# Output projections: the residual by plain loads and VectorE adds, and the linear attention's second block in the order of its first

## The chip, the cores and the metric

One core of a Trainium2 chip. The time of a kernel is device microseconds (us) of one execution of the whole program. The kernel before was run three times; its median is the time before. One further execution was taken by the hardware profiler, and everything said of the inside of the kernel is from that one. The engines are named as in the profile: PE (TensorE, matrix products; PEld is its loading of the stationary operand), DVE (VectorE), ACT (ScalarE), POOL (GpSimd) and SP (SyncE, which here only issues transfers).

## The reference

A decoder trunk of two layers for one sequence of 256 tokens, width 2048, all in float32. The first layer is a gated linear attention, the second a block-sparse attention (MoBA) over a shared K and V; behind each stands a gated convolutional FFN of hidden width 5632. Cut to what matters:

```python
def reference(x, ...):
    h = x
    for layer in range(2):
        if layer < 1:
            h = h + gla_mixer(h, ...)      # ends with  o.reshape(B, S, 2048) @ w_out
        else:
            k_blk, v_blk, k_mean = shared_kv(h, ...)
            h = h + moba_mixer(h, ...)     # ends with  o @ w_out
        h = h + conv_ffn(h, ...)           # ends with  (silu(a) * u) @ w_down
    return h
```

The change concerns the two products `@ w_out`, each of 256 x 2048 by 2048 x 2048, and the addition of `h` (the residual) to their results.

## The kernel before, in words

**Products.** A weight matrix is streamed from HBM in chunks of 1 MB (128 partitions x 2048 floats). SP issues the loads; the chunks go into three buffers (`raw`, tile `wraw`). Each chunk is split, in pieces of 1024 columns, into a high part (`whi`, a cast by ScalarE, L140) and a low part (`wlo`, a subtraction by VectorE, L141), both in the type that TensorE multiplies at full pace. The activations have been split in the same way. A product of two split numbers takes three matmuls: high x high, low x high and high x low. A `wraw` buffer is free for the next load only when the last cast and the last subtraction that read it are done. `WeightStream.prefetch` makes splits and loads a few pieces ahead of their use.

**Output and down projections (`down`, L702).** There are four: "go" (linear attention), "dn0", "mo" (MoBA) and "dn1". Each goes over two column blocks `b` of 1024 outputs. In a block, the 2048 (or 5632) inputs come as pairs of 128-row tiles, one chunk of weights for each pair. A pair is done in one of two ways:

- *plain*: 24 matmuls of 128x512, straight from the chunk's two wide pieces;
- *seven-product* (a `+` in the order): a 2x2 block scheme with 7 instead of 8 products, so 21 matmuls. Its chunk has four pieces: `b11` (half width), `wide`, and two sums of blocks, `t13` and `t24`, which VectorE computes first in three operations (`_sums`, L106 to L108; 1024, 512 and 512 elements a row), and which are then split like the other pieces. It also needs combined activations (`comb`).

The order of the pairs in each block stands in a table, `ORDERS`; what comes behind the bar is the block's *tail* of three plain pairs (20 and 21 pairs have theirs likewise in "dn0" and "dn1"). The matrix in HBM is packed in the order of the table.

Eight accumulators hold the partial results. At the last seven-product pair, five of them are merged into four tiles `r[0]` to `r[3]` (`c0` to `c3`, L756 to L760). In "go" and "mo" two of the others (`p[2]` and `p[3]`) are the halves of one accumulator pair (`acc`), and two (`p[4]` and `p[8]`) have a bank each. The tail runs twice over its three pairs: first for the column half `f = 0` (`p[2]`, `p[4]`), then for `f = 1` (`p[3]`, `p[8]`). Behind each half two results are added to their `r` (L771), and `done` (L781) takes the finished tile: a store (L784, GpSimd's queue), its squares for the next norm (L317, ScalarE), and later its transposes by TensorE (L795).

**The residual.** Right after the merge, four loads on GpSimd's queue add the residual to `r[0]` to `r[3]` in memory (L762, `accum_op=OP.add`): in "go" from `x_tok`, in "mo" from `rows2`, in the down projections from `rows1` and `rows3`. Each is 128 x 512 floats, 256 KB.

**What sets the order.** The program is written as one sequence; the framework's scheduler (switched on by `schedule_with_timeline_sim=True`) puts each engine's instructions in a fixed order before the run, and on the chip every engine and every queue works strictly in that order. `ws.behind()` keeps an instruction behind the latest split pieces. A moved dependency can so change the order on several engines around it.

Of the kernel before, what the change touches and what calls it, by code (L numbers as in the profile page):

```python
# [8 lines left out]
F32 = mybir.dt.float32  # L9
# [3 lines left out]
OP = mybir.AluOpType  # L13
# [24 lines left out]
def _order(text):  # L38

    words = text.replace("|", " ").split()  # L40
    return [(int(k.rstrip("+")), k.endswith("+")) for k in words], len(text.split("|")[1].split())
# [1 line left out]

EARLY = (1, 3, 5, 7)
ORDERS = {
    "go": [_order("0 1+ 2 3+ 4 | 5 6 7"), _order("0 2 1+ 3+ 4 | 5 6 7")],
    "dn0": [_order("0 2 4 6 8 1+ 10 3+ 12 5+ 14 7+ 16 9+ 17 11+ 18 13+ 15 | 19 20 21"),
            _order("0 2 4 6 1+ 8 3+ 10 5+ 12 7+ 14 9+ 16 11+ 13+ 18 15+ 17+ 19 | 20 21")],
    "mo": [_order("0 2 1+ 3+ 4 | 5 6 7"), _order("0 2 1+ 3+ 4 | 5 6 7")],
# [108 lines left out]
def trunk(ctx: ExitStack, tc: tile.TileContext, xT, x_tok, cst, msk, w1p, w2a, w_k, w_qa, w_v2, w_v, w_g, w_go,  # L158
          w_up0, w_dn0, w_kk, w_kv, w_mq, w_mo, w_up1, w_dn1, rel, onehot, out):
    nc = tc.nc  # L160
    V, A, T = nc.vector, nc.scalar, nc.tensor
# [11 lines left out]
    def slot(shape, dt, name):  # L173
        return big.tile(shape, dt, name=name, tag="slot")

    def temp(name, shape=(128, 2, S), dt=F32):
        return tmp.tile(list(shape), dt, name=name, tag="temp")

    def bank(name, shape):
        return mis_ps.tile(list(shape), F32, name=name, tag="bank")  # L180
# [5 lines left out]
    ws = WeightStream(tc, raw, parts)  # L186
# [85 lines left out]
    def step():  # L272
        due = [job for at, job in later if at <= cur[0]]
        later[:] = [(at, job) for at, job in later if at > cur[0]]
        for job in due:
            job()
        halves_ = ws.get(cur[0])
        cur[0] += 1
        return halves_
# [331 lines left out]
    def combine_parts(k, xs, into):  # L611
        t = temp("whole")
        V.tensor_add(t, xs[k][:, :, :S], xs[k][:, :, S:])
        combine(k, [(t[:, i, :128], t[:, i, 128:]) for i in range(2)], into)
# [4 lines left out]
    go, go_sums = [], {}  # L619
# [81 lines left out]

    def down(name, xs, combos, res, done, jobs):  # L702

        for b, (order, n_tail) in enumerate(ORDERS[name]):
            new = [k for k, seven in order if seven and k not in combos]
            todo = {i: list(js) for i, js in jobs.get(b, {}).items()}
            for k in new:
                at = next(i for i, (k_, _) in enumerate(order) if k_ == k)
                todo.setdefault(max(at - 2, 0), []).append(lambda k=k: combine_parts(k, xs, combos))
            low = acc_ps.tile([128, 2, 512], F32, name="acc")  # L710
            pair, single = ((3, 8), (2, 4)) if name.startswith("dn") else ((2, 3), (4, 8))
            p = {n: low[:, i] for i, n in enumerate(pair)}
            p.update({n: bank(f"p{n}", (128, 512)) for n in single})
            left = dict.fromkeys(range(1, 9), 0)
            for k, seven in order:
                for n in ((1, 5, 7, 6, 4, 3, 2) if seven else (2, 3, 4, 8, 2, 3, 4, 8)):
                    left[n] += 3
            begun = set()

            def prods(*todo):  # L720

                w = step()
                for n, _, _ in todo:
                    if n not in p:
                        two = acc_ps.tile([128, 2, 512], F32, name="acc")
                        p.update({n: two[:, 0], {1: 6, 5: 7}[n]: two[:, 1]})
                for xi, wi in ((0, 0), (1, 0), (0, 1)):
                    for n, x, f in todo:
                        left[n] -= 1
                        T.matmul(p[n], x[xi], w[wi][:, 512 * f:512 * f + 512], start=n not in begun, stop=left[n] == 0)  # L730
                        begun.add(n)

            def part(k, i, t):
                x = xs[k][:, i, 128 * t:]
                return x[:, :128], x[:, S:S + 128]

            def comb(k, f):
                return combos[k][:, f, 0], combos[k][:, f, 1]

            last = max(i for i, (k, seven) in enumerate(order) if seven)  # L740
            for i, (k, seven) in enumerate(order[:-n_tail]):
                for job in todo.get(i, ()):
                    job()
                if seven:
                    prods((1, part(k, 0, 0), 0))
                    prods((3, comb(k, 3), 0), (2, part(k, 1, 0), 1))
                    prods((5, comb(k, 0), 0), (7, comb(k, 2), 1))
                    prods((6, comb(k, 1), 0), (4, part(k, 1, 1), 1))
                else:
                    for a in range(2):  # L750
                        prods(*((n, part(k, a, t), f)
                                for n, t, f in ((2, 0, a), (3, 0, 1 - a), (4, 1, a), (8, 1, 1 - a))))
                if i == last:

                    r = [temp(f"c{n}", (128, 512)) for n in range(4)]
                    A.copy(r[0], p[1])  # L756
                    V.tensor_add(r[1], r[0], p[6])  # L757
                    V.tensor_add(r[2], r[1], p[7])
                    V.tensor_add(r[1], r[1], p[5])
                    V.tensor_add(r[3], r[2], p[5])  # L760
                    for n in (0, 2, 1, 3):
                        nc.gpsimd.dma_start(r[n], res(n // 2, 2 * b + n % 2), accum_op=OP.add)  # L762
            for f, ns in enumerate(((2, 4), (3, 8))):
                for i, (k, _) in enumerate(order[-n_tail:]):
                    for job in todo.get((f, i), ()):
                        job()
                    prods(*((n, part(k, a, t), a) for a in range(2) for t, n in enumerate(ns)))
                if f:
                    ws.prefetch(cur[0])
                for t, n in enumerate(ns):  # L770
                    V.tensor_add(r[2 * t + f], r[2 * t + f], p[n])  # L771
                    done(t, 2 * b + f, r[2 * t + f])
# [41 lines left out]
    def middle(name, xs, combos, res, nrm, keep_row, at, feature_major, parked=None):  # L814
        done, back, in_acc, in_bank = onward(nrm, keep_row, parked)
        jobs = {}
        for q, (b, i) in enumerate(at):
            jobs.setdefault(b, {}).setdefault(i, []).append(lambda q=q: back(q, in_acc))
        down(name, xs, combos, res, done, jobs)
        for q in range(len(at), NP):  # L820
            after(1 if feature_major else q - 3, lambda q=q: back(q, in_bank))
        after(2 if feature_major else 3, nrm.close)
        if feature_major:
            after(3, nrm.weave)
# [7 lines left out]
    def last_down(hid, sums):  # L832
        def done(t, c, x):
            (A if t and c % 2 else nc.sync).dma_start(out[t, :, 512 * c:512 * c + 512], x)

        down("dn1", hid, sums, rows3, done, {})
# [149 lines left out]
    for g in range(4):  # L986
# [4 lines left out]
        f = (q8[:, g % 2 * 4:g % 2 * 4 + 4], (q1[:, 0:2], q1[:, 2:4]))  # L991
# [3 lines left out]
    for g in range(4):  # L995
# [3 lines left out]
        f = (k8[:, g % 2 * 4:g % 2 * 4 + 4], [slot([128, 2, 2, S], F32R, f"k1{c}") for c in range(2)])  # L999
# [120 lines left out]
```

## Time and profile before

| what | value |
|---|---|
| median of 3 runs | 2191.21 us (2190.79 to 2191.95) |
| the profiled execution | 2188.61 us, of which the span of its instructions is 2186.7 |
| granted TensorE clock | 0.999 over the span |
| TensorE busy | 2170.4 us, 99% |
| VectorE, ScalarE, GpSimd busy | 1597.0, 1284.1 and 300.9 us |
| moved | 510.11 MB, mean 233 GB/s |

The profile is read as follows. A row of a timeline has the start in us, the time in us, the engine, the line of the kernel, the operation and the tiles (out<-in), how often, and in brackets the idle time before it with what ended it. A row of waits names who waited, for whom, the sum in us, the number and the longest. A row of groups ends with the busy time in us and the mean of one in ns, then the idle time before. A row of transfers has the count, the size of one and the median time in us from issue to landing. "DMA share" is the mean busy share of the core's 16 DMA engines. Line numbers in all rows of before are those of the code above. Matmuls are pipelined, so their single durations overlap; a wait that is not idle on the engine's own rows isn't seen there.

### The profile page before, as it was taken

To read this page: it belongs to the slowest core of one execution; us is meant where nothing else is said; L and a number is where in the kernel's file an instruction comes from. 1 tells how busy PE (TensorE), PEld (TensorE's weight loads), DVE (VectorE), ACT (ScalarE), POOL (GpSimd) and SP (SyncE) were. 2 spreads that over 40 slices of the span, in tenths; PEclk is the share of its full clock that TensorE was granted. 3 is DMA by queue.
4 is the path that set the end of the run, shared out by engine and by line. 5 is a ranking of instruction groups with operands and counts; after the bars stand their busy time and mean duration, and the time that the engine had idled before them with its cause. 6 is when DMAs were issued, how large, how long until landed. Compare 5 with 4: busy or idle time off the path is not lost.

```text
span 2186.7 us, 26956 instructions
## 1 busy us (share of the span) xinstructions
PE 2170.4 (99%) x9693; PEld 1793.1 (82%) x9693; DVE 1597.0 (73%) x2202; ACT 1284.1 (59%) x1858; POOL 300.9 (14%) x448
## 2 busy tenths in 40 slices
PE   9999999999999999999999999999999999999999
PEld 7888887888888888788888888888888888887887
DVE  6655586667776777878967787776777676769887
ACT  6555765556565656555556676555656565655454
POOL 1011111111111111000023241011111111110000
PEclk9999999999999999999999999999999999999999
DMA  8466577577777787675678887676687777775655
GB/s 317 178 231 210 185 245 256 201 241 232 240 240 242 242 256 234 198 251 202 223 252 269 275 277 229 205 235 230 232 249 236 247 237 246 237 243 206 222 205 173
DMA packets 92248, 510.11 MB, mean 233 GB/s; under 512 B 13729, under 2 KB 14769, under 8 KB 42194
## 3 DMA queue, kind: packets, MB, share of 16 engines
q1 hardware_dynamic: 60722, 417.53, 54.4%
q0 software_dynamic: 30816, 90.28, 15.3%
q8 instruction: 76, 1.25, 0.2%
q10 hardware_dynamic: 576, 0.58, 0.1%
q14 instruction: 58, 0.48, 0.1%
HBM read 463.22 MB, written 45.11 MB: 232 GB/s over the span
## 4 chain that ended last, share of the span: by engine, by line
PE 85%; DMA 5%; DVE 4%; issue 4%; ACT 1%; POOL 1%; DVEq 0%; SPq 0%; ACTq 0%; POOLq 0%
PE acc L290 41%; PE acc L293 20%; PE acc L730 13%; PE p L730 9%; DVE wlo L141 2%; DMA wraw<-w_dn 1%; DMA upT<-turned 1%; DMA wraw<-w_go 1%; ACT whi L140 1%; POOL upT L667 1%; DMA turned<-z 0%; PE sT L561 0%; DMA h<-xT 0%; PE o L578 0%; DVE au L680 0%
## 5 line engine op out<-in xcount | busy, mean ns | idle before, releaser
L141 DVE TENSOR_TENSOR wlo<-wraw,whi 128x1024 fp32r<-128x1024 f32 (+1 forms) x786 | 929.7, 1190 | 398.5 <-ACT whi L140 376.7
L140 ACT CAST whi<-wraw 128x1024 fp32r<-128x1024 f32 (+1 forms) x786 | 797.2, 1026 | 604.9 <-PE acc L290 391.0
L290 PE MATMUL acc<-whi,xw 128*128 128x512 f32 x3840 | 952.9, 390 | 2.6 <-ACT whi L140 1.9
L290 PEld LDWEIGHTS acc<-whi,xw 128*128 128x128 f32 x3840 | 719.5, 188 | 154.8 <-ACT whi L140 3.8
L293 PE MATMUL acc<-wlo,xw 128*128 128x512 f32 x1920 | 514.2, 389 | 0.0
L293 PEld LDWEIGHTS acc<-wlo,xw 128*128 128x128 f32 x1920 | 360.3, 188 | 74.8
L730 PE MATMUL p<-whi,hid 128*128 128x512 f32 x572 | 204.0, 390 | 0.0
L730 PE MATMUL acc<-whi,hid 128*128 128x512 f32 x506 | 168.8, 389 | 0.0
L676 ACT ACTIVATE au<-upT,cs 128x256 f32<-128x256 f32 x176 | 96.0, 595 | 70.1 <-DMA upT<-turned 70.1
L140 ACT CAST whi<-t 128x1024 fp32r<-128x1024 f32 x82 | 85.5, 1052 | 87.5 <-PE p L730 26.8
L667 POOL DMA_DIRECT2D upT<-turned x176 | 114.3, 656 | 148.7 <-DMA turned<-z 59.5
L290 PE MATMUL acc<-whi,xkv 128*128 128x512 f32 x512 | 128.8, 391 | 0.0
L661 POOL DMA_DIRECT2D turned<-z x44 | 34.1, 776 | 676.7 <-DVE z L657 615.0
L730 PEld LDWEIGHTS p<-whi,hid 128*128 128x128 f32 x572 | 107.4, 188 | 22.7 <-ACT whi L140 0.4
L680 DVE SCALAR_TENSOR_TENSOR au<-upT,cs,au 128x255 f32<-128x255 f32 x176 | 77.4, 471 | 55.8 <-ACT au L676 55.6
L730 PEld LDWEIGHTS acc<-whi,hid 128*128 128x128 f32 x506 | 95.0, 188 | 19.6
L730 PE MATMUL acc<-whi,comb 128*128 128x512 f32 x328 | 107.6, 393 | 3.4 <-ACT whi L140 3.1
L290 PEld LDWEIGHTS acc<-whi,xkv 128*128 128x128 f32 x512 | 94.6, 188 | 18.7
L730 PE MATMUL p<-wlo,hid 128*128 128x512 f32 x286 | 106.4, 391 | 2.6 <-DVE wlo L141 2.6
L141 DVE TENSOR_TENSOR wlo<-t,whi 128x1024 fp32r<-128x1024 f32 x82 | 98.6, 1217 | 9.8 <-ACT whi L140 5.4
L730 PE MATMUL acc<-wlo,hid 128*128 128x512 f32 x253 | 92.2, 389 | 0.0
L762 POOL DMA_DIRECT2D c<-rows x24 | 21.3, 1074 | 463.4 <-DVE c L757 451.2
(251 smaller groups left out, 1956.3 us busy)
## 6 DMA issues: line engine op xcount, KB each, us to landing
wraw<-w_up SPq DMA_DIRECT2D x176, 1024.0 KB, 5.3
wraw<-w_dn SPq DMA_DIRECT2D x88, 1024.0 KB, 4.9
turned<-z POOLq DMA_DIRECT2D x44, 512.0 KB, 3.5
upT<-turned POOLq DMA_DIRECT2D x176, 128.0 KB, 5.0
wraw<-w_g SPq DMA_DIRECT2D x16, 1024.0 KB, 5.0
wraw<-w_go SPq DMA_DIRECT2D x16, 1024.0 KB, 5.4
wraw<-w_mq SPq DMA_DIRECT2D x16, 1024.0 KB, 6.6
wraw<-w_kk SPq DMA_DIRECT2D x16, 1024.0 KB, 6.0
```

The costliest lines, as they stand in the source:

```text
L140: one = nc.scalar.copy(hi[:, a:b], src[:, a:b])
L141: two = nc.vector.tensor_sub(lo[:, a:b], src[:, a:b], hi[:, a:b].bitcast(F32))
L290: T.matmul(ps[:, t, :], xs(kt)[:, x0 + 128 * t:x0 + 128 * t + 128], hi[:, c:c + 512], start=kt == 0 and x0 == 0, stop=False)
L293: T.matmul(ps[:, t, :], xs(kt)[:, 128 * t:128 * t + 128], lo[:, c:c + 512], start=False, stop=kt == KT - 1)
L661: nc.gpsimd.dma_start(turned[J].rearrange("(a i) r q c -> (i r) a (q c)", a=4), z.rearrange("p (a q) t c -> p a (q t c)", a=4))
L667: nc.gpsimd.dma_start(f[32 * q:32 * q + 32].rearrange("p a (i c) -> p (a i) c", i=4), turned[J][:, :, q, :].rearrange("a r c -> r a c"))
L676: A.activation(au[:, i, :], t[:, i, :], AF.Identity, bias=col(cb + n), scale=col(cw + 2 * 2 * FT + n))
L680: V.scalar_tensor_tensor(au[:, i, 1:], t[:, i, :S - 1], col(cw + 2 * FT + n), au[:, i, 1:], op0=OP.mult, op1=OP.add)
L730: T.matmul(p[n], x[xi], w[wi][:, 512 * f:512 * f + 512], start=n not in begun, stop=left[n] == 0)
L762: nc.gpsimd.dma_start(r[n], res(n // 2, 2 * b + n % 2), accum_op=OP.add)
```

## The change

Three things.

1. In "go" and "mo" the residual's four accumulating loads of a block are replaced by four plain loads into two new tiles, `kept` (one for each half `f`, 128 x 2 x 512). They stand in the program ahead of the merge. "dn0" and "dn1" keep their accumulating loads.
2. In the tail, after the first of the three pairs of each half, two VectorE operations add the half's `kept` to its two `r` (now L777), behind the latest split pieces. That makes 4 in a block, 16 in all.
3. The order of block 1 of "go" becomes that of block 0: the seven-product pairs 1 and 3 are no longer next to each other. The number of matmuls, of loads of weights and of sums stays.

```diff
     "go": [_order("0 1+ 2 3+ 4 | 5 6 7"), 
-           _order("0 2 1+ 3+ 4 | 5 6 7")],
+           _order("0 1+ 2 3+ 4 | 5 6 7")],
...
     def down(name, xs, combos, res, done, jobs):
+        loaded = name in ("go", "mo")
...
                 if i == last:
+                    kept = [slot([128, 2, 512], F32, "kept") for _ in range(2)] if loaded else []
+                    for f, x in enumerate(kept):
+                        for t in range(2):
+                            nc.gpsimd.dma_start(x[:, t], res(t, 2 * b + f))
                     r = [temp(f"c{n}", (128, 512)) for n in range(4)]
                     A.copy(r[0], p[1])
                     V.tensor_add(r[1], r[0], p[6])
                     V.tensor_add(r[2], r[1], p[7])
                     V.tensor_add(r[1], r[1], p[5])
                     V.tensor_add(r[3], r[2], p[5])
-                    for n in (0, 2, 1, 3):
-                        nc.gpsimd.dma_start(r[n], res(n // 2, 2 * b + n % 2), accum_op=OP.add)
+                    if not loaded:
+                        for n in (0, 2, 1, 3):
+                            nc.gpsimd.dma_start(r[n], res(n // 2, 2 * b + n % 2), accum_op=OP.add)
             for f, ns in enumerate(((2, 4), (3, 8))):
                 for i, (k, _) in enumerate(order[-n_tail:]):
...
                     prods(*((n, part(k, a, t), a) for a in range(2) for t, n in enumerate(ns)))
+                    if i == 0 and loaded:
+                        with ws.behind():
+                            for t in range(2):
+                                V.tensor_add(r[2 * t + f], r[2 * t + f], kept[f][:, t])
```

What this makes of the engines' orders is shown at three places. All are in the linear attention's output projection ("go"), where block 0's tail ends and block 1 begins. The numbers behind the tiles' names only tell buffers apart, and differ between the two programs; lines from L731 on are shifted too.

**VectorE, from the last splits of block 0 on.** `go_2625` (in the change `go_2627`) is the last pair's activations, `wlo_2645` (`wlo_2652`) the low part of block 0's last piece of weights, and c0 the first finished result (L771, now L781). `wraw_2608` (`wraw_2610`) is block 1's second chunk. Before:

```order
L304 TENSOR_TENSOR go_2601<-g_2598,go_2601 128x2x256
L141 TENSOR_TENSOR wlo_2605<-wraw_2487,whi_2604 128x1024
L141 TENSOR_TENSOR wlo_2668<-wraw_2567,whi_2667 128x1024
L304 TENSOR_TENSOR go_2625<-g_2622,go_2625 128x2x256
L141 TENSOR_TENSOR wlo_2645<-wraw_2548,whi_2644 128x1024
L771 TENSOR_TENSOR c0_2585<-c0_2585,acc_2420 128x512
L771 TENSOR_TENSOR c2_2587<-c2_2587,p4_2421 128x512
L141 TENSOR_TENSOR wlo_2710<-wraw_2608,whi_2709 128x1024
```

Now:

```order
L304 TENSOR_TENSOR go_2627<-g_2624,go_2627 128x2x256
L141 TENSOR_TENSOR wlo_2672<-wraw_2567,whi_2671 128x1024
L106 TENSOR_TENSOR t13_2630<-wraw_2610 128x1024
L107 TENSOR_TENSOR t24_2631<-t13_2630,wraw_2610 128x512
L141 TENSOR_TENSOR wlo_2714<-wraw_2610,whi_2713 128x512
L777 TENSOR_TENSOR c1_2592<-c1_2592,kept_2586 128x512
L777 TENSOR_TENSOR c3_2594<-c3_2594,kept_2586 128x512
L108 TENSOR_TENSOR t24_2631<-wraw_2610,t24_2631 128x512
L141 TENSOR_TENSOR wlo_2652<-wraw_2548,whi_2651 128x1024
L777 TENSOR_TENSOR c0_2591<-c0_2591,kept_2585 128x512
L777 TENSOR_TENSOR c2_2593<-c2_2593,kept_2585 128x512
L141 TENSOR_TENSOR wlo_2688<-wraw_2567,whi_2687 128x1024
```

Six operations now stand ahead of block 0's last low part (`wlo_2652`) that did not stand there before: the three sums of block 1's second chunk, one narrow low part of it, and two of the new adds. Behind the last row shown stands one more wide low part (`wlo_2732`), and then c0 at L781.

**TensorE, at the end of block 0's tail.** These are the products with the last piece (`whi_2651`, `wlo_2652`) into `p8`, then those into `acc_2420`, whose other half holds the result that c0 takes. In the change:

```order
L731 MATMUL p8_2422<-whi_2651,go_2627 128x512 [waits Activation_49]
L731 MATMUL p8_2422<-whi_2651,go_2627 128x512 x3
L731 MATMUL p8_2422<-wlo_2652,go_2627 128x512 [waits DVE_49]
L731 MATMUL p8_2422<-wlo_2652,go_2627 128x512
L731 MATMUL acc_2420<-whi_2606,go_2499 128x512 [waits DVE_49]
L731 MATMUL acc_2420<-whi_2606,go_2499 128x512 x3
L731 MATMUL acc_2420<-wlo_2607,go_2499 128x512 x2
```

Before, the first products with block 0's last piece (then `whi_2644`) and their wait on ScalarE stood ten rows earlier; the third row and what follows it, with the waits on VectorE in the third and the fifth, stand as they did. The fifth row's wait is for c0.

**GpSimd's queue, around the residual.** Before:

```order
L393 DMA turned_2452<-gates_1554 32x4x256 x4
L762 DMA c0_2585<-x_tok 128x512
L762 DMA c1_2586<-x_tok 128x512
L762 DMA c2_2587<-x_tok 128x512
L762 DMA c3_2588<-x_tok 128x512
L784 DMA rows1_2415<-c0_2585 128x512
```

Now:

```order
L393 DMA turned_2452<-gates_1554 32x4x256 x4
L759 DMA kept_2585<-x_tok 128x512 x2
L759 DMA kept_2586<-x_tok 128x512 x2
L794 DMA rows1_2415<-c0_2591 128x512
L794 DMA rows1_2415<-c3_2594 128x512
```

The place in the queue is the same, behind the last "turned" loads; what the loads write, and so what they wait for, is another. In "mo" the order of TensorE's products stays, and the plain loads and adds come in the same way.

More of the change, by code (lines that the diff above doesn't have):

```diff
@@ L45 @@
 ORDERS = {
-    "go": [_order("0 1+ 2 3+ 4 | 5 6 7"), _order("0 2 1+ 3+ 4 | 5 6 7")],
+    "go": [_order("0 1+ 2 3+ 4 | 5 6 7"), _order("0 1+ 2 3+ 4 | 5 6 7")],
     "dn0": [_order("0 2 4 6 8 1+ 10 3+ 12 5+ 14 7+ 16 9+ 17 11+ 18 13+ 15 | 19 20 21"),
```

## Prediction

> **What bounds the kernel now.** I read the page first, then TensorE's own waits, then the place of the longest: its timeline, the chain of waits that leads there, and a table of stretches.
>
> ```profile
> PE 2170.4 (99%) x9693; PEld 1793.1 (82%) x9693; DVE 1597.0 (73%) x2202; ACT 1284.1 (59%) x1858; POOL 300.9 (14%) x448
> ```
> ```profile
> PE acc L730 <- ACT whi L140: 3.1, 1, 3.1
> PE p L730 <- DVE wlo L141: 3.1, 4, 0.9
> ```
>
> TensorE is idle for some 16 us of 2186.7. The change adds and removes no matmul, so it can move only waits. The longest single one, 3.1 us, lies in block 1 of the linear attention's output projection:
>
> ```profile
> 346.18 0.62 PE L730 MATMUL p<-wlo,go 128*128 128x512 f32 x2
> 349.91 0.50 PE L730 MATMUL acc<-whi,comb 128*128 128x512 f32 x1 [3.12 <-ACT whi L140]
> ```
> ```profile
> 291.90:328.60 36.70, 36.70 (x163) 30.41 (x162) 31.25 (x35) 23.06 (x32) 6.34 (x9) 1.00 0.76 245
> 320.00:326.00 6.00, 6.00 (x28) 4.96 (x27) 5.45 (x6) 3.92 (x6) 2.04 (x3) 1.00 0.86 132
> 326.00:333.00 7.00, 7.00 (x33) 5.76 (x32) 2.16 (x3) 1.96 (x4) 1.15 (x2) 1.00 0.99 372
> 351.30:354.70 3.40, 3.40 (x8) 2.70 (x9) 3.40 (x5) 2.71 (x3) 0.00 (x0) 0.50 0.52 173
> 354.70:358.10 3.40, 3.40 (x16) 2.79 (x15) 3.19 (x3) 1.47 (x2) 0.00 (x0) 1.00 1.00 400
> ```
>
> A row of this table has the stretch, its length, the busy time of TensorE, its weight loads, VectorE, ScalarE and GpSimd, then the granted clock, the DMA share and GB/s. After the wait the clock is 0.50 for 3.4 us, and TensorE issues 8 matmuls where the next such stretch has 16: 8 × 0.227 = 1.8 us more. (0.227 us is the pace of a matmul: 36.70 us for 162 of them, worked out below.) The wait itself costs 349.91 − 346.18 − 2 × 0.227 = 3.3 us. Together **5.1 us**.
>
> What was late is told by the chain of waits up to that place (start, us, what):
>
> ```profile
> 322.59 8.36 DMA wraw<-w_go
> ...
> 331.04 1.06 ACT whi L140
> ...
> 338.04 7.21 DMA wraw<-w_go
> ...
> 346.70 1.15 DVE t L106
> ...
> 347.87 1.99 ACT whi L140 x2
> ```
>
> The weights of block 1's second pair are issued at 322.59 and take 8.4 us. ScalarE, in its written order, has that pair's cast ahead of older ones, so it stands still until 331; the buffer of block 1's first pair is given back late, the load at 338.04 starts late, and its casts are ahead of the one TensorE waits for. Beside the 8.4 us stand the accumulating loads:
>
> ```profile
> 317.95 0.94 POOL L762 DMA_DIRECT2D c<-x_tok  x1 [11.24 <-DVE c L757]
> 319.39 2.65 POOL L762 DMA_DIRECT2D c<-x_tok  x3 [0.49 <-DVE c L759]
> ```
> ```profile
> wraw<-w_mo SPq DMA_DIRECT2D x16, 1024.0 KB, 4.9
> ...
> c<-x_tok POOLq DMA_DIRECT2D x8, 256.0 KB, 7.0
> ```
>
> From 320 to 326 the DMA engines are 0.86 busy for only 132 GB/s; with weights, 0.99 for 372. A load of weights by itself takes 4.9 us, here 3.5 more.
>
> **The change part by part.** *Accumulating loads become plain ones, GpSimd's queue.* They no longer wait for the sums (the 11.24 us above); the queue has them right behind the last "turned" loads, so they start near 307 and not at 318 to 321. The DMA time of four (1.05 MB) is 1.05 / (132 / 0.86) = 6.8 us now. Plain rows of 2 KB have no row by themselves: at the weights' rate they take 1.05 / (372 / 0.99) = 2.8 us; if accumulation costs nothing, 6.8. I take 2.8, since the same queue moves plain data well. Where they go the engines are full already:
>
> ```profile
> 306.00:318.00 12.00, 12.00 (x55) 9.94 (x54) 10.42 (x11) 8.97 (x12) 0.76 (x3) 1.00 0.99 359
> ```
>
> so weights that are due there come 0 to 2.8 us later. I take 1.4 for the load that matters below. Gone are the 3.5 us on the load at 322.59, and with them the cause of the wait at 346.18: **−5.1 us**.
>
> *Sixteen adds on VectorE.* One of this form, from SBUF alone:
>
> ```profile
> L304 DVE TENSOR_TENSOR go<-g,go 128x512 fp32r<-128x512 f32 x4 | 2.7, 685 | 0.0
> ```
>
> 16 × 0.69 = 11 us of VectorE, 2.7 in each of four tails. The engine is 73% busy, and in 326 to 333 it works 2.16 us of 7, so as a sum they are covered. What is not covered is where they stand, below.
>
> *Block 1's new order.* As many matmuls and bytes as before. The second chunk of weights now belongs to a seven-product pair, so sums (L106 to L108) are due as soon as it lands. The rows shown with the change put these, and all four new adds, **ahead** of two things that TensorE needs: the low part of block 0's last weights (wlo_2652; its counterpart stood right behind the "go" split) and the first add of block 0's results (c0, now L781), before which TensorE may not write the other half of that accumulator. In the trace both came early:
>
> ```profile
> 321.34 2.37 DVE L141 TENSOR_TENSOR wlo<-wraw,whi 128x1024 fp32r<-128x1024 f32 x2
> ...
> 324.23 1.22 DVE L141 TENSOR_TENSOR wlo<-wraw,whi 128x1024 fp32r<-128x1024 f32 x1
> 329.06 0.69 DVE L771 TENSOR_TENSOR c<-c,acc 128x512 f32<-128x512 f32 x1 [3.61 <-PE acc L730]
> ...
> 333.86 1.22 DVE L106 TENSOR_TENSOR t<-wraw 128x1024 f32<-128x1024 f32 x1
> 335.00 0.69 DVE L141 TENSOR_TENSOR wlo<-wraw,whi 128x512 fp32r<-128x512 f32 x1
> 335.60 0.68 DVE L107 TENSOR_TENSOR t<-t,wraw 128x512 f32<-128x512 f32 x1
> 336.20 0.68 DVE L771 TENSOR_TENSOR c<-c,acc 128x512 f32<-128x512 f32 x1
> ```
>
> From start to start a wide operation (1024) takes 1.14 us, a narrow one (512) 0.60. When does TensorE need them? Block 0 begins here:
>
> ```profile
> 291.91 0.62 PE L730 MATMUL acc<-whi,go 128*128 128x512 f32 x2
> ...
> 294.63 0.62 PE L730 MATMUL acc<-whi,go 128*128 128x512 f32 x2
> ```
>
> 12 matmuls in 2.72 us, 0.227 each. A plain pair has 24, a seven-product pair 21, the tail 72: 3 × 24 + 2 × 21 + 72 = 186. In the new order 24 of them are still to come when TensorE reaches the products with block 0's last weights (4 with the high part, 2 with the low, then 12 and 6 into the other accumulator), so it is there at 291.91 + 162 × 0.227 = 328.6 (the first table row shows no idle time up to there) and would need c0 at 328.6 + 6 × 0.227 = 330.0.
>
> When are they there? The load of block 1's second chunk is released by the same VectorE operation as before, the first of the two at 321.34, and issued at 322.6. Undisturbed it lands at 322.6 + 4.9 = 327.5; with my 1.4 at 328.9; at the latest at 330.3. From the landing VectorE does, in the new order: L106 1.14, L107 0.60, a narrow low part 0.60, two adds 1.20, L108 0.60; then wlo_2652, which ends 4.14 + 1.22 = 5.4 us after the landing, at 334.3. Behind it two adds 1.20 and two wide low parts 2.28, then c0: it starts 8.76 and ends 9.4 us after the landing, at 338.3. TensorE would have gone on at 330.0: **+8.3 us** (6.9 with the earliest landing, 9.7 with the latest). An earlier landing yet would not help: the narrow low part takes a buffer that TensorE reads until 328.6, which leaves at least 6.5.
>
> These waits come as one of some 4 and one of 4 us, with two matmuls between them. The only wait of over 2 us here, 3.12, was followed by half clock for 3.4 us, so I put **+1.8 us** on it; below nothing lies no reason, the upper end is two such stretches, 3.6. [...]
>
> In block 1, TensorE is then some 8 us later against its loads, and the third and fourth chunks, released by wlo_2652 and the wide low part behind it, are issued near 334 and 337 and used from 349 on: covered by 10 us.
>
> *The attention's projection.* Its order is unchanged; its adds stand behind low parts that are ready, not behind a landing, and its accumulating loads caused no wait of over 0.9 us. I cost it at nothing. If the cover fails: its plain loads start near 1386, where the engines are full, ahead of a TensorE wait on low parts,
>
> ```profile
> 1386.00:1388.00 2.00, 2.00 (x10) 1.65 (x9) 0.91 (x1) 0.83 (x2) 0.00 (x0) 1.00 1.01 410
> 1396.00:1400.00 4.00, 3.41 (x19) 2.48 (x18) 3.61 (x4) 3.58 (x5) 0.00 (x0) 1.00 0.03 8
> ```
>
> and could make that one up to 2.8 us longer.
>
> **Sum**: −5.1 + 8.3 + 1.8 = **+5.0 us** on the profiled execution's 2188.6, 2193.6. The runs shown have a median of 2191.2, 2.6 above it, which I carry along: **2196.2 us**. Ends: 6.5 − 5.1 + 0 = +1.4 (2192.6) and 9.7 − 5.1 + 3.6 = +8.2 (2199.4).
>
> **The rivals.** About 0.2% (4.4 us) is what a measurement here can tell from no change.
>
> *One wait for another, even.* The new wait at its lower end without half clock (+1.4), or a wait in the ordinary runs that is longer than in the profiled execution: these are 2.6 us slower for a reason I don't see, and if that is the accumulating loads, the change removes 7.7: 5.0 − 2.6 = +2.4. 2192.6 to 2195.6. For it: the 2.6. Against: the spread of the runs is 1.2, so it would be always there.
>
> *Faster.* The old wait goes and no new one comes: 2191.2 − 5.1 = 2186.1. It decides from the point where VectorE's chain ends by 330.0, which a landing at 320.6 would need, before the load is issued; or where TensorE doesn't wait for c0. For it: the DMA time is truly freed. Against: the rows of the order.
>
> *Slower by more.* The plain loads among full queues hold up the tail's own weights, and the attention's wait grows by 2.8: 2196.2 + 2.8 = 2199.0 and above. For it: shares of 0.99 and 1.01. Against: the casts have 5 us of lead in the tail.
>
> *Nothing happens*, both kinds of loads being hidden: 2191.2. Against it the wait at 349.91.
>
> **How the numbers follow.** Forecast 0.52, even 0.26, faster 0.08, slower by more 0.10, nothing 0.04. Of the forecast 0.46 lies above the bound of 2195.6: slower 0.46 + 0.10 = 0.56; same 0.06 + 0.26 + 0.04 = 0.36; faster 0.08. The range from 2189 to 2200.5 leaves out the faster case and part of the slowest. The forecast's own is 2192.6 to 2199.4.
>
> **What would show it.** No TensorE wait near 350 and half clock not there; in its place two waits between 329 and 339, the first ended by VectorE's low part (L141), the second by L781; half clock within 340 to 345; plain loads issued near 307; a load of weights issued near 322.6 that lands by 329. Wrong it is if TensorE passes 330 without a wait, if the attention's projection has a new one, or if the last chunks of block 1 are waited for.

## The result

The change makes the kernel slower. The median is 2202.9 us (6 runs, 2198.7 to 2207.8), before 2191.6 us (6 runs, 2190.8 to 2195.9); the ratio is **1.0056, 95% interval 1.0043 to 1.0070**, so about 12 us. In a later run of the same two programs it was 1.0035 (1.0022 to 1.0047), about 8 us. The forecast was +5.0 us, and 2202.9 lies above the end of its range, 2200.5.

The profiled execution of the changed kernel took 2207.4 us, with a span of 2205.5; it is one of the longer ones. Its page and TensorE's waits (who waited, for whom; us in all, times, longest):

```profile
PE 2177.3 (99%) x9693; PEld 1795.5 (81%) x9693; DVE 1607.4 (73%) x2218; ACT 1284.2 (58%) x1858; POOL 294.9 (13%) x448
```
```profile
PE acc L290 <- ACT whi L140: 5.6, 6, 2.8
PE p L731 <- DVE wlo L141: 5.0, 5, 1.8
PE acc L731 <- ACT go L303: 3.8, 1, 3.8
PE acc L731 <- DVE c L781: 3.3, 1, 3.3
```

The old wait (on ScalarE's `whi`, 3.1 us near 346, L730 then) is gone. The fourth row is the forecast wait for c0, and 1.8 of the second that for the low part. The third row, on the cast of "go", and the first, 4.1 us of it in the first FFN's up projection, were not forecast (of the first row 1.9 us were there before). In TensorE's timeline (start, us, ..., idle before and what ended it):

```profile
319.76 0.39 PE L731 MATMUL p<-wlo,go 128*128 128x512 f32 x1
323.99 0.79 PE L731 MATMUL acc<-whi,go 128*128 128x512 f32 x1 [3.84 <-ACT go L303]
...
335.74 1.21 PE L731 MATMUL p<-whi,go 128*128 128x512 f32 x4 [0.75 <-ACT whi L140]
338.79 0.73 PE L731 MATMUL p<-wlo,go 128*128 128x512 f32 x2 [1.83 <-DVE wlo L141]
342.86 2.07 PE L731 MATMUL acc<-whi,go 128*128 128x512 f32 x4 [3.34 <-DVE c L781]
```

The table of stretches, with the granted clock and the DMA share behind the engines' busy times, shows half clock twice in this projection, 6.8 us each:

```profile
322.70:329.50 6.80, 5.51 (x13) 4.36 (x14) 5.71 (x7) 4.52 (x8) 0.00 (x0) 0.50 0.26 86
...
339.80:346.60 6.80, 3.74 (x9) 2.97 (x10) 4.20 (x6) 1.44 (x4) 1.64 (x3) 0.50 0.95 349
346.60:353.40 6.80, 6.80 (x34) 5.56 (x33) 3.27 (x5) 4.05 (x8) 2.68 (x5) 1.00 0.86 274
```

**Where the time went.** All profiles have the same 9693 matmuls, so the starts of matmuls with the same number can be compared, in the order of TensorE's rows. From no. 1420 (in block 0's tail) to no. 1700 (behind block 1) and from no. 1750 to 3850 (the first FFN's up projection), in us, from the traces of all kernels that are told of below:

```
                                            1420-1700   1750-3850
before                                          66.84      476.85
changed                                         76.71      483.31
changed, second profile                         73.91      478.32
changed, loads at the second pair               74.82      481.89
old order, all eight loads at the first pair    74.10      477.38
plain loads and adds, old order                 69.03      480.15
new order alone                                 69.64      476.72
changed, without block 0's loads                72.00      476.00
plain loads and adds in MoBA alone              66.64      476.00
new order and adds, no loads ("go")             73.23      476.00
old order, adds, no loads ("go")                64.57      476.00
old order, block 0's loads on SyncE's queue     65.20      476.00
before, pieces in program order                 64.07      476.00
no loads ("go"), pieces in program order        65.99      476.00
```

The output projection accounts for +9.9 of the profiled execution's difference, the up projection for +6.5 (waits of 1.25 us up to 507.8 and of 2.81 us up to 599.0, and 3.4 us of half clock behind the second); the second down projection (from no. 8650 to the last) took 242.1 against 239.7, where the other profiles lie between 238.0 and 241.2. The second profile of the same program has +7.1 and +1.5, so a good part of the 19 us between the two spans belongs to that one execution. Within the projection, by the starts of the same matmuls: +4.0 at the wait near 320 and +2.7 by half clock behind it; +0.9, +2.0 and +3.5 at the three waits from 335 to 343 and +1.8 by half clock behind them; −5.3 where the old wait was. That is +9.6, and 0.3 lies scattered.

### The profile page after: what moved, and what is told of

Its sections match the earlier page's. It is cut to its first block, busy times and chain, and to the rows that moved or that the text cites. A ratio compares the mean times of both kernels' runs of the same rounds, so it can differ in the third digit from the quotient of the medians.

```text
span 2205.5 us, 26973 instructions
## 1 busy us (share of the span) xinstructions
PE 2177.3 (99%) x9693; PEld 1795.5 (81%) x9693; DVE 1607.4 (73%) x2218; ACT 1284.2 (58%) x1858; POOL 294.9 (13%) x448
## 3 DMA queue, kind: packets, MB, share of 16 engines
q0 software_dynamic: 29792, 90.28, 14.7%
q8 instruction: 76, 1.25, 0.2%
## 4 chain that ended last, share of the span: by engine, by line
PE 87%; issue 5%; DMA 5%; DVE 2%; ACT 1%; POOL 0%; SPq 0%; DVEq 0%; ACTq 0%; POOLq 0%
PE acc L290 43%; PE acc L293 21%; PE acc L731 12%; PE p L731 8%; DMA upT<-turned 2%; DVE wlo L141 1%; DMA wraw<-w_dn 1%; ACT whi L140 0%; DMA c<-rows 0%; DMA wraw<-w_go 0%; DMA w2s<-w2a 0%; PE sT L561 0%; POOL upT L667 0%; PE o L578 0%; PE acc L805 0%
## 5 line engine op out<-in xcount | busy, mean ns | idle before, releaser
L731 PE MATMUL p<-whi,hid 128*128 128x512 f32 x572 | 204.1, 390 | 0.0
L731 PE MATMUL acc<-whi,hid 128*128 128x512 f32 x506 | 168.8, 389 | 0.0
L731 PEld LDWEIGHTS p<-whi,hid 128*128 128x128 f32 x572 | 107.4, 188 | 22.7 <-ACT whi L140 0.4
L731 PEld LDWEIGHTS acc<-whi,hid 128*128 128x128 f32 x506 | 95.0, 188 | 19.6
L731 PE MATMUL p<-wlo,hid 128*128 128x512 f32 x286 | 106.4, 391 | 2.6 <-DVE wlo L141 2.6
L731 PE MATMUL acc<-whi,comb 128*128 128x512 f32 x328 | 106.7, 390 | 0.8 <-ACT whi L140 0.7
L731 PE MATMUL acc<-wlo,hid 128*128 128x512 f32 x253 | 92.2, 389 | 0.0
L682 DVE SCALAR_TENSOR_TENSOR au<-upT,cs,au 128x254 f32<-128x254 f32 x176 | 80.1, 477 | 0.0
```

Source lines behind the costliest of these rows:

```text
L682: V.scalar_tensor_tensor(au[:, i, 2:], t[:, i, :S - 2], col(cw + n), au[:, i, 2:], op0=OP.mult, op1=OP.add)
```

## The experiments

Ratios are to the kernel before on the same chip, with the 95% interval; 1% is 21.9 us. The first theory (A) was that the plain loads, right beside the weights of block 0's tail, make the wait near 320.

**Plain loads and adds without the new order.**

```diff
-    "go": [_order("0 1+ 2 3+ 4 | 5 6 7"), _order("0 1+ 2 3+ 4 | 5 6 7")],
+    "go": [_order("0 1+ 2 3+ 4 | 5 6 7"), _order("0 2 1+ 3+ 4 | 5 6 7")],
```

> The change without its third part: plain loads and VectorE adds in both output projections, block 1 of the linear attention's in the order it had before. Theory A (the plain loads, issued near 307 with the tail's own weights, delay the load of weights issued at 308.6, and with it a cast that is ahead of the activations TensorE waits for at 320): the wait of 4.0 us near 320 and the half clock behind it (2.7 us lost) stay, the chain of sums at 334 to 343 does not come, and the old wait near 346 (5.3 us with its half clock) goes: 2191.6 + 6.7 - 5.3 = 2193.0 us. Rival B (the wait near 320 was an accident of the profiled execution or comes from the new order): no wait near 320, 2186.3 us.

Measured: 1.0030 (1.0018 to 1.0041), 6.5 us slower. The wait near 320 is there, without half clock behind it, and, against both theories, so is the old one:

```profile
322.44 0.50 PE L731 MATMUL acc<-whi,go 128*128 128x512 f32 x1 [2.51 <-ACT go L303]
...
351.77 0.55 PE L731 MATMUL acc<-whi,comb 128*128 128x512 f32 x1 [2.88 <-ACT whi L140]
```

So the old wait does not need the accumulating loads. In the chain ahead of it here stands again a load of weights that took long, now beside block 1's plain loads:

```profile
339.07 8.04 DMA wraw<-w_go
```

In this profile the projection takes 2.2 us longer than before, and the up projection 3.3.

**The new order alone**, with accumulating loads:

```diff
-    "go": [_order("0 1+ 2 3+ 4 | 5 6 7"), _order("0 2 1+ 3+ 4 | 5 6 7")],
+    "go": [_order("0 1+ 2 3+ 4 | 5 6 7"), _order("0 1+ 2 3+ 4 | 5 6 7")],
```

> The change's third part alone: accumulating loads as before, block 1 of the linear attention's projection in the order of block 0. Theory A: no wait near 320. The sums of block 1's second chunk are still ahead of block 0's last low part on VectorE, and the accumulating loads still delay that chunk (8.4 us, landing near 331): its low part ends 5.4 us later at 336.4, where TensorE needs it at 329.5: one wait of near 6.9 us with 1.8 to 3.5 us of half clock; the old wait near 346 (5.3) goes: 2191.6 + 8.7 - 5.3 = 2195.0 us (up to 2196.7). Rival (the sixteen adds are what makes VectorE's chain late, the order itself costs nothing): 2186.3 us.

Measured: 1.0003 (0.9994 to 1.0012), no difference. The old wait is gone, with the accumulating loads still there. In its place is one wait, with 6.8 us of half clock (0.50 from 332.7 to 339.5). ScalarE ends it, since the load of block 1's second chunk took 8.3 us:

```profile
334.77 2.07 PE L730 MATMUL p<-whi,go 128*128 128x512 f32 x4 [4.32 <-ACT whi L140]
```
```profile
324.78 8.28 DMA wraw<-w_go
```

On VectorE c0 stands here ahead of the low part of block 0's last weights, so there is no second wait for it. Both expectations were off: within the interval, the order costs what it saves.

**The change without block 0's plain loads** (and so without the residual in the first 1024 outputs of this projection):

```diff
-                            nc.gpsimd.dma_start(x[:, t], res(t, 2 * b + f))
+                            if name == "go" and b == 0:
+                                nc.gpsimd.memset(x[:, t], 0.0)
+                            else:
+                                nc.gpsimd.dma_start(x[:, t], res(t, 2 * b + f))
```

> The changed kernel without the four plain loads of block 0 of the linear attention's projection: GpSimd fills the two kept tiles with zeros instead, so this block's outputs lack the residual; the adds stay. Theory A: no wait near 320, block 1's second chunk is issued near 322.6 and lands by 327.5, and what was forecast of the order remains: waits of 0.9, 2 to 3 and 3.5 us between 329 and 339, half clock 1.8, the old wait gone: 2191.6 + 4.5 = 2196.1 us. Rival B (the load of weights issued at 308.6 is slow for another reason): the wait near 320 stays, 2203 us.

Measured: 1.0019 (1.0010 to 1.0028), 4.2 us slower, as theory A has it. What was forecast of the order is there almost to the number:

```profile
322.51 0.50 PE L731 MATMUL acc<-whi,go 128*128 128x512 f32 x1 [1.20 <-ACT go L303]
...
331.74 1.20 PE L731 MATMUL p<-whi,go 128*128 128x512 f32 x4 [0.75 <-ACT whi L140]
335.56 1.08 PE L731 MATMUL p<-wlo,go 128*128 128x512 f32 x2 [2.62 <-DVE wlo L141]
339.63 1.65 PE L731 MATMUL acc<-whi,go 128*128 128x512 f32 x3 [3.00 <-DVE c L784]
```

A wait near 320 of 1.2 us is left, which the profile of before does not have; the run with the order alone had one of 1.1 us. At this place the kernel has little slack, whatever is loaded.

**MoBA's part alone** (`loaded = name == "mo"`, old order in "go"):

> Plain loads and VectorE adds in MoBA's output projection alone, the linear attention's as before. Theory A (nothing in MoBA's projection is late enough to be seen): 2191.6 us, the wait of 5.3 us near 346 still there, no wait over 1 us in MoBA's projection. Rival C (half of the loss is MoBA's, or comes later from it): 2195 us or more.

Measured: 0.9994 (0.9985 to 1.0003). MoBA's projection takes the same time (90.5 us from its first product to its last, before 90.7), no wait in it is over 0.6 us, and the old wait near 346 is still there (3.3 us). The loss comes from the change in the linear attention's.

**The change once more, its loads earlier, and eight loads earlier.** Three runs on one chip; in the second the plain loads stand at each block's second pair, in the third all eight of "go" at its first pair, with the old order:

```diff
...
+                if i == 1 and loaded:
+                    kept = [slot([128, 2, 512], F32, "kept") for _ in range(2)]
+                    for f, x in enumerate(kept):
+                        for t in range(2):
+                            nc.gpsimd.dma_start(x[:, t], res(t, 2 * b + f))
```

> The changed kernel once more, for a second profile beside its neighbours here: 1.0056 of the time before, some 12 us more. The wait near 320 of about 4 us and the three waits between 334 and 343 are there again. Open is what the 6.5 us in the first FFN's up projection were (two waits near 506 and 596): theory S, they are scatter, then that stage takes near 476 us as in four other profiles, or waits at other places; theory T, the change causes them, then it takes over 479 us with waits at these same places.

> The changed kernel with its plain loads put into the program at the second pair of each block and not at the last seven-product pair, so that block 0's four stand in GpSimd's queue ahead of the last turned loads and run from 302 on, where the DMA engines were 0.30 busy; order and adds as changed. Theory A (the plain loads' place costs the wait near 320): the load of weights issued near 309 lands within 7 us, the wait near 320 is at most 1.4 us, and the waits behind it stay: +4 us against the kernel before, as in the run without block 0's loads. Rival B (the four loads cost as much wherever they stand, since the turned loads are then late): +11 us.

> Block 1 in its order of before; in the linear attention's projection the plain loads of both blocks (eight) are put at the projection's first pair, from 302 on. MoBA's part as changed. Theory D (the old wait near 346 comes from transfers beside the weights issued at 322.6 and 339: accumulating loads before, block 1's plain loads in the run with plain loads alone): neither is there now, the load near 322.6 takes about 5 us, the wait near 346 is under 1 us, none near 320: 5 us faster than before. Rival E (the old wait comes from the written order of the casts alone): it stays at 3 us or more, no difference from before, or 2 us slower by late turned loads.

Measured: 1.0035 (1.0022 to 1.0047), 1.0052 (1.0040 to 1.0065) and 1.0033 (1.0021 to 1.0046). In the second profile of the change the three waits between 333 and 342 are the same; the one near 320 is 1.9 us and not 4, with 3.4 us of half clock behind it. The up projection took 478.3 us there, with the wait near 506 but without that near 596, so it fits neither theory S nor theory T as they were put. Loads placed earlier in the program did not help. They were issued only from 304.6 and from 302.7 on, behind a store that waits for its data, and ahead of the last "turned" loads; the tail's weights were then later still. In the chain of the third:

```profile
312.68 12.71 DMA wraw<-w_go
...
327.37 0.63 ACT go L303
328.00 0.04 issue
328.04 0.80 PE acc L731
```

Rival B of the second run holds: four loads on that queue cost as much a little earlier. In the third run the wait ahead of 328 is 6.7 us long, and 2.2 us of the old wait are still there, though the residual's loads had all landed by 320. That speaks for rival E, at less than the 3 us it named.

**The residual without any load**: the input lies in SBUF from the start (four tiles that the first norm uses), and "go" adds it from there, in the old order.

```diff
-                    kept = [slot([128, 2, 512], F32, "kept") for _ in range(2)] if loaded else []
+                    kept = xt[2 * b:2 * b + 2] if name == "go" else []
...
```

> Block 1 in its order of before; the linear attention's projection adds the residual from the tiles in which the input was loaded at the start (four tiles kept for it until then), with no load at all beside its weights. MoBA's part as changed. Theory D: no wait over 1.4 us near 320, the load near 322.6 takes about 5 us, the wait near 346 is under 1 us: 5 us faster than before. Rival E: the wait near 346 stays: no difference. Rival F (four of 35 slots held for 300 us delay others): new waits ahead of 290, slower.

Measured: 0.9990 (0.9981 to 0.9999), 2 us faster than before. No wait over 1 us near 320, and the load near 322.6 takes 4.8 us. But with no load of the residual beside the weights, most of the old wait is still there; the half clock behind it is gone:

```profile
349.04 0.50 PE L731 MATMUL acc<-whi,comb 128*128 128x512 f32 x1 [2.35 <-ACT whi L140]
```

So rival E fits 2.4 of the 3.1 us idle: the wait would be in the written order, which the last experiment tests. ScalarE and VectorE have pieces of block 1's *second* seven-product pair ahead of the first pair's wide piece, and so TensorE waits for a load that it doesn't need yet.

**The new order and adds without loads** in "go":

> The changed kernel's order and adds, the linear attention's residual from the tiles of the start (no loads beside its weights); MoBA's part as changed. It leaves the price of order and adds by themselves, for both blocks: as in the run without block 0's loads, waits of 0.9, 2.8 and 3.4 us between 329 and 340 with 2 us of half clock, the old wait gone: +4 us against before. Rival: without block 1's loads too, less than half of that.

Measured: 1.0018 (1.0009 to 1.0027), 3.9 us slower. That is the price of order and adds. The run with the order alone had +0.7, some 3 us less (the intervals are ±2 us each), but it also had the accumulating loads, so the price of the adds by themselves is not shown.

**Block 0's four plain loads on SyncE's queue**, in the old order:

```diff
-                            nc.gpsimd.dma_start(x[:, t], res(t, 2 * b + f))
+                            (nc.sync if name == "go" and b == 0 else nc.gpsimd).dma_start(x[:, t], res(t, 2 * b + f))
```

> Plain loads and adds in block 1's order of before, with block 0's four plain loads on SyncE's queue, where they stand behind the last of that block's weights (issued near 317), and not on GpSimd's beside them. Theory A (the loads' place among the tail's weights makes the wait near 320): that wait is at most 1.5 us. On the first FFN's up projection: if the slow store there (7 to 9 us in all five profiles with these four loads on GpSimd's queue, 3.5 to 5.1 in the others) follows from that queue, it takes 5 us or less here and the stage near 476 us; if it follows from the plain loads as such, it is slow again. In all +1 to +2 us against before, the old wait near 348 still there.

Measured: 0.9995 (0.9986 to 1.0004). Behind the tail's weights in the weights' own queue the same four loads cost nothing: no wait near 320, and the up projection takes 476.0 us. Against the same loads on GpSimd's queue (1.0030) that is 7.7 us by the two ratios; in the profiles 1.2 us of it lie at the old wait, which half clock does not follow here. The loads are also issued later, from 314.2 on and not from 306.2. Which of the two helps, the other queue or the later time, no run separates.

**The pieces in their program's order**, on the kernel before and on the version that has the residual in SBUF. In `prefetch`, for block 1 of "go":

```diff
+                    if n in self.strict:
+                        for ins in self.latest:
+                            order.enter_context(self.tc.issue_after(ins))
                     one = nc.scalar.copy(hi[:, a:b], src[:, a:b])
...
```

The subtraction behind it is put under the same rule.

> The kernel before, with one thing added: in block 1 of the linear attention's projection the split pieces of the seven-product pairs are kept in their program's order on ScalarE and VectorE (the second pair's pieces no longer ahead of the first pair's wide piece). The accumulating loads stay. Theory G (the old wait near 346 comes from that written order): it is under 1 us, no half clock there: 5 us faster than before, 0.2%. Rival H (it comes from the accumulating loads and the late chunk they cause): 3 us or more remain.

> The same order of pieces, on top of the version that adds the residual from the tiles of the start. Theory G: the 2.6 us near 346 that were left go: about 5 us faster than before. Rival H: the transfers were the rest, nothing more is gained than that version's 3 us; or the order makes a new wait elsewhere in block 1.

Measured: **0.9977 (0.9968 to 0.9987)**, 5.0 us faster than before, and 0.9986 (0.9978 to 0.9995). The first is as theory G has it, and the fastest of all versions; 0.57 us are left of the old wait, at full clock (lines are shifted by the edit):

```profile
349.91 0.50 PE L737 MATMUL acc<-wlo,comb 128*128 128x512 f32 x1 [0.57 <-DVE wlo L148]
```

The order is what was meant. ScalarE's half-width cast of the second pair, which waited for its load ahead of the first pair's wide piece, stands behind it now; before:

```profile
345.36 0.62 ACT L140 CAST whi<-wraw 128x512 fp32r<-128x512 f32 x1 [4.70 <-DMA wraw<-w_go]
```

Now the wide piece:

```profile
346.77 1.04 ACT L147 CAST whi<-wraw 128x1024 fp32r<-128x1024 f32 x1
```

The accumulating loads are all in it, and the load issued at 324.7 beside them still takes 8.3 us: a slow load there costs nothing by itself. By the starts of the matmuls 4.3 us go at the old wait; a new wait of 1.2 us near 320 takes part of that back, so that this profile's projection gains 2.8 us and its span 4.1.

The second run is not as theory G has it, but as rival H: 3.1 us and not 5, about what the version without loads had by itself. The old wait is down to 0.3 us, but waits of 1.15 us near 320 and of 0.85 us at 351 and 0.87 us at 384 came with the order. Taking the accumulating loads away as well gains nothing that can be measured.

## Why the prediction was wrong, and where it was right

**"Gone are the 3.5 us on the load at 322.59, and with them the cause of the wait at 346.18: −5.1 us."** The size was right in the changed kernel (−5.3), the reason wrong. The wait stayed without the accumulating loads (2.88 us, half clock behind it) and went with them in place (the order alone; the strict order, where the load beside them is as slow as it was). Its cause is the written order of the split pieces. I had seen in the chain that ScalarE stood still ahead of older casts, but took the slow load, which made it worse, for the cause. In the change it was the new order of the pairs that removed it.

**"Weights that are due there come 0 to 2.8 us later. I take 1.4 for the load that matters below."** This is the step that failed. The load that mattered was not that at 322.6 (it is issued at 326.6 now and lands in 4.6 us), but one in the tail itself. The chain of waits of the changed kernel, ahead of the wait near 320:

```profile
308.63 10.05 DMA wraw<-w_go
...
318.76 1.06 ACT whi L140
...
323.32 0.63 ACT go L303
323.94 0.04 issue
323.99 0.79 PE acc L731
```

Before, the same load took 5.7 us and its cast began at 314.74, as that kernel's chain of waits shows (start, length, piece):

```profile
308.99 5.68 DMA wraw<-w_go
...
314.74 1.06 ACT whi L140
```

The load ends at 314.67, and ScalarE's cast follows at once. GpSimd's four loads are issued in one go, just ahead of it:

```profile
306.95 2.19 POOL L759 DMA_DIRECT2D kept<-x_tok  x4
```

The next load of the tail, issued at 311.9, is late too: it takes 9.4 us, before 5.0. The cast of "go" stands behind those of the weights on ScalarE, and TensorE needs it at 320. In the rivals I wrote "the casts have 5 us of lead in the tail". I had no row for that. Two rows of before, ScalarE's cast and the product that needs it, give the lead:

```profile
319.13 0.62 ACT L303 CAST go<-g 128x512 fp32r<-128x512 f32 x1
```
```profile
320.47 0.39 PE L730 MATMUL acc<-whi,go 128*128 128x512 f32 x1
```

The cast ends at 319.75, so the lead is 0.7 us. In the change the cast began 4.2 us later (323.32 − 319.13) and TensorE was 0.5 us earlier; it waited 4.0. That rival, "slower by more", had the right mechanism, but with a price of 2.8 us taken from MoBA's projection, and a chance of 0.10. With 6.7 us (4.0 and 2.7 of half clock) put to the sum, the forecast is +11.7, and the profile's projection shows +9.9, the rest being mostly the next point. How large the term is varies: in the second profile it is 3.8 us (2.0 and 1.8 of half clock), and the projection shows +7.1.

**"+8.3 us" and "+1.8 us" for VectorE's chain.** Right in mechanism and place: the timeline of VectorE is the chain as forecast.

```profile
331.27 1.23 DVE L106 TENSOR_TENSOR t<-wraw 128x1024 f32<-128x1024 f32 x1 [2.72 <-DMA wraw<-w_go]
332.53 0.69 DVE L107 TENSOR_TENSOR t<-t,wraw 128x512 f32<-128x512 f32 x1
335.10 0.69 DVE L141 TENSOR_TENSOR wlo<-wraw,whi 128x512 fp32r<-128x512 f32 x1 [1.88 <-PE p L731]
335.71 1.28 DVE L777 TENSOR_TENSOR c<-c,kept 128x512 f32<-128x512 f32 x2
336.91 0.68 DVE L108 TENSOR_TENSOR t<-wraw,t 128x512 f32<-128x512 f32 x1
337.51 1.22 DVE L141 TENSOR_TENSOR wlo<-wraw,whi 128x1024 fp32r<-128x1024 f32 x1
338.65 1.29 DVE L777 TENSOR_TENSOR c<-c,kept 128x512 f32<-128x512 f32 x2
339.85 2.35 DVE L141 TENSOR_TENSOR wlo<-wraw,whi 128x1024 fp32r<-128x1024 f32 x2
342.12 0.68 DVE L781 TENSOR_TENSOR c<-c,acc 128x512 f32<-128x512 f32 x1
```

The waits came to 6.4 us (0.9, 2.0, 3.5), near the lower bound of 6.5 that the text worked out (from its own steps it is 328.6 + 7.7 − 330.0 = 6.3): the narrow low part waited for the buffer that TensorE read (1.88 idle, the third row). A wait of 0.9 for ScalarE's high part was not forecast as one of its own. Half clock cost 1.8, as taken. In the run without block 0's loads the waits were 7.1 us, its projection +5.2: the forecast +5.0 was the forecast of that kernel.

**"I cost it at nothing"** (MoBA): right, by the run with MoBA's part alone.

**Nothing was forecast for the up projection.** In all five profiles with block 0's plain loads on GpSimd's queue its fourth store took 7.2 to 8.9 us from issue to landing, in the other profiles 3.5 to 5.1, and TensorE then waits once or more. GpSimd's rows of the changed kernel at this place:

```profile
487.02 0.78 POOL L661 DMA_DIRECT2D turned<-z  x1 [16.80 <-DVE au L682]
496.16 2.59 POOL L667 DMA_DIRECT2D upT<-turned  x4 [8.35 <-PE acc L293]
```

And of the run with these loads on SyncE's queue:

```profile
476.00 0.78 POOL L661 DMA_DIRECT2D turned<-z  x1 [14.91 <-DVE z L657]
482.00 2.59 POOL L667 DMA_DIRECT2D upT<-turned  x4 [5.23 <-issue]
```

The loads behind the store are issued 9.1 us after it in the one and 6.0 in the other. In the first, TensorE's row is

```profile
507.83 1.43 PE L290 MATMUL acc<-whi,xw 128*128 128x512 f32 x5 [1.25 <-ACT whi L140]
```

The stage took 477.4 to 483.3 us in these five, 476.0 to 476.9 in the others. That it goes with block 0's plain loads on that queue is shown by the runs: with the same loads on SyncE's queue it is gone. Why a store 170 us later is struck is not. In the changed kernel it is issued 1.9 us after its data is ready, in the run without block 0's loads 0.3; its first packet starts 3.5 to 3.8 us after the issue in the five, 1.35 in the others. A rival is untested: in the five traces 5008 packets had started on GpSimd's queue before this store, in the others 5520, 4688 or 4368, so it may be the count on that queue and not the loads as such. This stays open.

## What to carry to other kernels

A wait that shows a slow transfer in its chain may still be one of order: ask whether the engine that stood still had to do that piece next; here a few lines that keep the pieces in order gained 5.0 us, and no transfer had to go. For a load of low urgency, try the place behind the urgent ones in their own queue: here it cost nothing there (0.9995 of the time before), and 6.5 us on a second queue beside them and earlier. And a lead that a sum relies on needs a row of the profile: the 5 us of lead in the tail were 0.7.

## What was unexpected of the hardware

- In these traces half clock did not follow the length of a wait alone. Idle times of 2.9 us (plain loads, old order) and 3.1 us (before) were followed by 3.4 us of it, one of 3.1 us (loads on SyncE's queue) was not. One of 1.9 us (near 320 in the second profile of the change) was, one of 2.5 us (near 320 with plain loads in the old order) was not. The stretch behind the first of these:

```profile
352.10:355.50 3.40, 3.40 (x9) 2.60 (x8) 3.40 (x5) 3.40 (x4) 0.00 (x0) 0.50 0.24 58
```

  The wait with loads on SyncE's queue, and the stretch that holds its end:

```profile
351.46 0.50 PE L731 MATMUL acc<-whi,comb 128*128 128x512 f32 x1 [3.07 <-ACT whi L140]
```
```profile
351.00:355.00 4.00, 3.41 (x14) 2.49 (x15) 4.00 (x6) 4.00 (x6) 0.00 (x0) 1.00 0.20 33
```

  In the output projection a stretch of half clock lasted 3.4 us (before, and plain loads in the old order) or 6.8 us (the change, and the new order alone). What decides whether one comes behind a wait is not shown.
- Plain loads were probably not quite as cheap on the DMA engines as taken. The page's row for this queue is, before and after:

```profile
q0 software_dynamic: 30816, 90.28, 15.3%
```
```profile
q0 software_dynamic: 29792, 90.28, 14.7%
```

  15.3% of 2186.7 less 14.7% of 2205.5 is 10 us for sixteen loads, 2.6 for four, with up to 0.6 of rounding: an estimate of 4.2 us for four plain loads where the accumulating ones took 6.8. With the second profile (14.6% of 2196.9) it is 14 us and 3.5, so 3.3 for four. The text had taken 2.8.
